# A two-layer retention and RWKV-7 backbone on one core: the values' products of each scan half step issued behind the products of the half step in front, in one PSUM bank for a pair of heads

## The chip, the cores and the metric

The kernel runs on one core of a Trainium2 chip. The metric is the device time of one execution in microseconds (us). The kernel before took 2461.8 us, the median of 3 runs (2458.17 to 2465.19).

## The reference

Two layers work on 1024 latent tokens and 256 context tokens of width 1024. Each layer normalizes, projects once to 4224 columns, runs two groups of heads, and sends both through one output projection. The group that matters here is the delta rule scan, 8 heads of 64 channels, in two directions, context first and then latents:

```python
def rwkv7_scan(r, w, k, v, kap, a, s0, reverse):
    def step(s, inp):
        r_t, w_t, k_t, v_t, kap_t, a_t = inp
        s_kap = jnp.einsum('bhvk,bhk->bhv', s, kap_t)
        s = (s * w_t[:, :, None, :]
             - s_kap[..., None] * (kap_t * a_t)[:, :, None, :]
             + v_t[..., None] * k_t[:, :, None, :])
        return s, jnp.einsum('bhvk,bhk->bhv', s, r_t)
    s_fin, y = lax.scan(step, s0, xs, reverse=reverse)
```

Around it, per layer:

```python
pl = hl @ w_in[layer]                       # and pc = hc @ w_in[layer] for the context
ret_l, ret_c = retention_branch(...)        # 8 retention heads, chunks of 128
rwo_l, rwo_c = rwkv_branch(...)             # the scan above, readout norm, bonus
mix_l = jnp.concatenate([ret_l * silu(gr_l), rwo_l * silu(gw_l)], axis=-1) @ w_out[layer]
xl = xl + g_l[:, None] * mix_l
```

## The kernel before

The scan is done in chunks. The 1280 tokens are 10 tiles of 128, the 8 heads are 4 pairs, so a layer has 40 steps (pair p, step s), and a step has two half steps of 64 tokens (i = 0 and 1). Both heads of a pair (h) and both directions (d) go through a half step together.

`prep` and `prep2` (called by `ahead`, up to three steps ahead of the scan) make what a half step needs without the state: `own` and `bk` (decayed keys and queries), `gq` (masked products of them), `bt` (transposed keys), `z2` (the inverse of the chunk's triangle, by six levels of small f16 products in the PSUM tile `pinv`), and `uv`. `uv` holds the values of a chunk, loaded by DMA, in partitions 64 to 127, and has two buffers.

`seq` (L1046) runs the scan. A half step takes a PSUM bank `pseq`, of which there is one (`sq=1`), seen as four regions k = 0 to 3, and in the text below each of its six groups of four f32 products (two heads, two directions) is called a set:

- v, the values' part: `gq` times `uv` into region 0 (L1053)
- s, the state's part: `own` times the state `st` into region 0, which ACT copies to `w` (L1068)
- w: `z2` times `w` into region 1; ACT and DVE copy it to `uv`, partitions 0 to 63 (L1080, L1081)
- a second s set, `own` times `st` for the outputs, into region 3
- b: `bt` times `uv` into region 2, from which DVE makes the next state `st` (L1093, two instructions)
- y: `gq` times `uv` into region 3, which ACT or DVE adds to the outputs `ym` (L1102, L1098)

All but v go through the helper `more` and carry its line, L1061. The first product of a set v clears the bank's written bits, and `behind` keeps the others of the bank after it in PE's order. Since the bank is taken anew for each half step, set v waits until the reads of the half step in front (L1093, L1098, L1102) are over.

The v and the y and b products take 128 rows by 64 columns of the array (64 columns per head, tile shape 128*64 in the rows), the s and w products 64*64, and nearly everything else 128*128 or 64*128.

Everything else is filler between the half steps: projections (`pproj`, L493 to L495, three f16 products for each f32 one), the retention heads (`pss`, `pkt`), the output projection (`pout`, L821 to L823). The program is scheduled by the tile framework, which plays it through with its own estimates and gives each engine a fixed order; `seq` and `prep2` are given a lead of 1000 places (`tc.high_priority(offset=1000)`), and `deal` hands out filler so that it ends at given steps. Each engine then works through its order.

Between the layers `out_last` adds the last output blocks for the tile groups [0,1], [4,5,6,7], [3,8] and [2,9], turns the residual (`pxo`, L890), and `norm_chunk` spreads the norm factors (`prsb`, L345) and writes `h_hi` and `h_lo`, on which layer 1's first projections work.

```python
with tc.high_priority(offset=1000):
    st = seq(sp, stages.pop(g), stages.get(g + 1) if s + 1 < NT else None, st, ys)
ahead(g + LOOK + 1)
```

Of the kernel before, what the change touches and what calls it, by code (L numbers as in the profile page):

```python
# [125 lines left out]
def hybrid_kernel(ctx: ExitStack, tc: tile.TileContext, a: dict, out: bass.AP, dbg: dict | None = None):  # L126
    nc = tc.nc
# [11 lines left out]
    def bank(tag, name):  # L139
        return ps.tile([128, 512], F32, tag=tag, name=name, bufs=BANKS[tag])  # L140
# [6 lines left out]
    def behind(ins, first):  # L147
        tc.add_manual_dep(ins.ins, first.ins.name, mybir.DependencyInfo(mybir.DependencyClass.NoSync, mybir.DependencyReason.DATA),
                          reason="the first product of a bank clears its written bits")
# [15 lines left out]
    def x_tile(tb):  # L165
        t = ln_pool.tile([128, D], F32, tag="xt", name="xt", bufs=XTB)
        load(t, a["ctx"][0, 128 * tb:128 * tb + 128, :] if tb < 2 else a["x"][0, 128 * (tb - 2):128 * (tb - 2) + 128, :])
        return t
# [39 lines left out]
    at = {}  # L208
# [162 lines left out]
    h = None  # L371
    rss, xres = {}, {}

    for l in range(DEPTH):
# [53 lines left out]
        h = (hp.tile([128, 8, TOK], F16, name="h_hi"), hp.tile([128, 8, TOK], F16, name="h_lo"))  # L428
        h_hi, h_lo = h
        if l == 0:  # L430
            lp = ln_pool
            stage = [lp.tile([128, 8, 128 * len(tiles)], F32, name=f"xs{ci}") for ci, tiles in enumerate(LN_TILES)]
            for ci, tiles in enumerate(LN_TILES):
# [5 lines left out]
                for i, tb in enumerate(tiles):  # L439
                    t = x_tiles[tb] if tb < XTB else x_tile(tb)  # L440
# [7 lines left out]
                for k in range(8):  # L448
                    p = bank(("inv", "m")[k % 2], "pxt")
# [457 lines left out]
        HR = [slice(0, 64), slice(64, 128)]  # L907
# [42 lines left out]
        def prep2(sp, c):  # L950
# [89 lines left out]
            nc.scalar.copy(z2, q)  # L1040
            c.update(gq=gq, bt=bt, z2=z2)

        def seq(sp, cur, nxt, st, ys):
            s, uv, gq, bt, z2, own = cur["s"], cur["uv"], cur["gq"], cur["bt"], cur["z2"], cur["own"]
            if s == 0:
                st = sp.tile([128, 2, 64], F32, tag="st", name="st", bufs=3)  # L1046
                nc.gpsimd.memset(st, 0.0)
            for i in range(2):
                pq = bank("sq", "pseq").rearrange("p (k d t) -> p k d t", k=4, d=2)
                first = []  # L1050
                for d in range(2):
                    for h in range(2):
                        wm = nc.tensor.matmul(pq[HR[h], 0, d, :], gq[:, h, i, d, 0:64], uv[:, i, d, 64 * h:64 * h + 64],  # L1053
                                              start=(d == 0), stop=False, skip_group_check=True)
                        if d == 0:
                            first.append(wm)
                        else:
                            behind(wm, first[h])

                def more(k, h, d, lhs, rhs, stop=False):  # L1060
                    rm = nc.tensor.matmul(pq[HR[h], k, d, :], lhs, rhs, start=False, stop=stop, skip_group_check=True)  # L1061
                    behind(rm, first[h])

                for d in range(2):
                    for h in range(2):
                        more(0, h, d, own[HR[h], i, d, 0:64], st[HR[h], d, :], True)
                w = sp.tile([128, 2, 64], F32, tag="w", name="w", bufs=2)
                nc.scalar.copy(w, pq[:, 0])  # L1068
                for d in range(2):
                    for h in range(2):  # L1070
                        more(1, h, d, z2[HR[h], i, d, :], w[HR[h], d, :], True)
                nf = cur["f"][:, 1, :] if i == 0 else (nxt["f"][:, 0, :] if nxt is not None else None)
                if nf is not None:
                    sf = sp.tile([128, 2, 64], F32, tag="sf", name="sf", bufs=1)
                    nc.gpsimd.tensor_tensor(sf, st, nf.unsqueeze(2).to_broadcast([128, 2, 64]), ALU.mult)
                for d in range(2):
                    for h in range(2):
                        if not cur["skip_y"]:
                            more(3, h, d, own[HR[h], i, d, 64:128], st[HR[h], d, :])
                nc.scalar.copy(uv[0:64, i, :, 0:64], pq[0:64, 1])  # L1080
                nc.vector.tensor_copy(uv[0:64, i, :, 64:128], pq[64:128, 1])  # L1081
                for d in range(2):
                    for h in range(2):
                        if nf is not None:
                            more(2, h, d, bt[:, i, d, 64 * h:64 * h + 64], uv[:, i, d, 64 * h:64 * h + 64], True)
                for d in range(2):
                    for h in range(2):
                        if not cur["skip_y"]:
                            more(3, h, d, gq[:, h, i, d, 64:128], uv[:, i, d, 64 * h:64 * h + 64], True)
                if nf is not None:  # L1090
                    st = sp.tile([128, 2, 64], F32, tag="st", name="st", bufs=3)
                    for d in range(2):
                        nc.vector.scalar_tensor_tensor(st[:, d, :], pq[:, 2, d, :], nf[:, d:d + 1], sf[:, d, :], ALU.mult, ALU.add)  # L1093
                if not cur["skip_y"]:
                    for d in range(2):
                        m, c = orders[d][s], (i if d == 0 else 1 - i)
                        if (m, c) in ys:
                            nc.vector.tensor_tensor(ys[m][:, c, :], pq[:, 3, d, :], ys[m][:, c, :], ALU.add)  # L1098
                        else:
                            if m not in ys:  # L1100
                                ys[m] = sp.tile([128, 2, 64], F32, tag="ym", name="ym", bufs=10)
                            nc.scalar.copy(ys[m][:, c, :], pq[:, 3, d, :])  # L1102
                        ys[(m, c)] = True
            return st
# [152 lines left out]
        for p in range(NP):  # L1257
            st, ys = None, {}
            for s in range(NT):
                g = p * NT + s  # L1260
# [3 lines that stand above are left out]
                if s == 1 and not last:  # L1264
                    need(p, gated)
                    readout(sp, p, s, 0, 1, ys)
                if s >= 6:
                    need(p, gated)
                    readout(sp, p, s, 11 - s, s, ys)
                deal(g)  # L1270
                while p == NP - 1 and not fills and todo and max(todo[0]) <= max(s, 1 if s < 7 else 7):
                    out_last(todo.pop(0))
# [43 lines left out]
```

## Time and profile before

| what | value |
|---|---|
| median of 3 runs | 2461.8 us (2458.17 to 2465.19) |
| the profiled execution | 2462.74 us |
| its span, first to last instruction | 2460.7 us |
| mean granted TensorE clock | 0.964 |
| busy: PE, DVE, ACT, POOL | 2299.2, 1735.6, 1414.8, 1319.7 us |
| products of the scan's sets in the trace (two records for each f32 product) | 1280 v, 2432 s, 1280 w, 1216 b, 1152 y |

The times of runs and of the profiled execution are of the whole device execution; the span leaves out 2.0 us around it. PE is TensorE, busy 93% of the span, and a busy PE may be one at half clock. The rows are times on one execution.

### The profile page before, as it was taken

How to read it: one execution, taken by the hardware profiler on the slowest of the kernel's cores; microseconds unless marked ns; L12 is line 12 of the kernel's file. 1: busy time of each engine (PE TensorE's matmuls, PEld its weight loads, DVE VectorE, ACT ScalarE, POOL GpSimd, SP SyncE). 2: the span in 40 equal slices, each digit the busy share in tenths (PEclk: the TensorE clock that was granted, in tenths of full speed). 3: DMA queues.
4: the chain of work that ended last, by engine and by line, in shares of the span. 5: the costliest groups of instructions: out<-in, count | busy, mean ns of one | idle time of the engine just before them, and what ended most of it. 6: DMA issues, size and time to landing. Idle time of an engine off the chain costs nothing.

```text
span 2460.7 us, 69593 instructions
## 1 busy us (share of the span) xinstructions
PE 2299.2 (93%) x25463; PEld 1739.9 (71%) x25463; DVE 1735.6 (71%) x4784; ACT 1414.8 (57%) x4261; POOL 1319.7 (54%) x2032
## 2 busy tenths in 40 slices
PE   5779999999999999999997899999999999998997
PEld 2357776877788777778655687778768877776855
DVE  2646686787678867777648677767867886669756
ACT  3455664565566655456546666646655665456663
POOL 1455564465556654456536556545654665456662
PEclk7888999999999999999998899999999999999998
DMA  8754443334334423335533543434433443334544
GB/s 313 270 187 110 117 118 87 113 108 124 78 89 139 126 70 92 75 100 154 176 108 123 152 130 112 108 94 119 128 87 100 124 124 80 79 88 120 143 130 128
DMA packets 539606, 302.77 MB, mean 123 GB/s; under 512 B 238995, under 2 KB 526465, under 8 KB 537217
## 3 DMA queue, kind: packets, MB, share of 16 engines
q1 hardware_dynamic: 539264, 298.33, 42.1%
q8 instruction: 201, 3.29, 0.6%
q14 instruction: 141, 1.15, 0.2%
HBM read 212.21 MB, written 85.98 MB: 121 GB/s over the span
## 4 chain that ended last, share of the span: by engine, by line
PE 58%; DVE 13%; DMA 6%; ACT 4%; issue 3%; POOL 2%; SPq 2%; DVEq 0%; POOLq 0%; ACTq 0%
PE pproj L493 8%; PE pproj L495 8%; PE pproj L494 8%; PE pseq L1061 8%; PE pm L962 5%; DMA ft<-feat 2%; PE pseq L1053 2%; PE pinv L1001 2%; PE pinv L1017 2%; PE pout L821 1%; PE pout L823 1%; PE pss L638 1%; PE pout L822 1%; PE pss L648 1%; PE pyt L1127 1%
## 5 line engine op out<-in xcount | busy, mean ns | idle before, releaser
L493 PE MATMUL pproj<-h_hi,whi 128*128 128x256 f16 (+2 forms) x2128 | 631.3, 298 | 9.1 <-ACT craw L505 5.1
L494 PE MATMUL pproj<-h_lo,whi 128*128 128x256 f16 (+2 forms) x2128 | 629.1, 297 | 7.6 <-DVE h_lo L365 7.1
L495 PE MATMUL pproj<-h_hi,wlo 128*128 128x256 f16 (+2 forms) x2128 | 627.2, 297 | 0.7 <-POOL wlo L320 0.7
L320 POOL TENSOR_TENSOR wlo<-wraw,whi 128x256 f16<-128x256 f32 x360 | 250.5, 707 | 208.7 <-ACT wraw L319 181.0
L495 PEld LDWEIGHTS <-wlo 128*128 128x128 f16 x2128 | 213.5, 100 | 76.5 <-issue 12.1
L494 PEld LDWEIGHTS <-whi 128*128 128x128 f16 x2128 | 212.6, 100 | 77.6 <-issue 18.6
L493 PEld LDWEIGHTS <-whi 128*128 128x128 f16 x2128 | 213.1, 100 | 75.3 <-issue 10.4
L986 POOL COPY ttb<-tt 64x256 f16<-64x256 f16 x320 | 139.1, 436 | 205.2 <-DVE tt L1021 160.5
L1015 DVE TENSOR_TENSOR xx<-pinv,lvm 128x256 f16<-128x256 f32 x400 | 164.3, 416 | 90.6 <-PE pinv L1001 87.4
L318 ACT ACTIVATE whi<-wraw 128x256 f16<-128x256 f32 x360 | 139.2, 412 | 132.9 <-PE pproj L494 61.1
L1018 ACT CAST tz<-pinv 128x256 f16<-128x256 f32 x400 | 146.1, 370 | 119.9 <-PE pinv L1017 107.7
L962 PE MATMUL pm<-own,bk 64*128 64x128 f32 (+1 forms) x1280 | 201.6, 294 | 8.3 <-DVE bk L942 4.0
L1021 DVE STREAM_TRANSPOSE tt<-tz 128x256 f16<-128x256 f16 x320 | 139.4, 437 | 97.0 <-ACT tz L1018 94.3
L976 POOL TENSOR_TENSOR il<-gq,c_id 64x256 f32<-64x256 f32 x160 | 120.1, 751 | 133.1 <-DVE gq L965 119.3
L986 ACT COPY ttb<-tt 64x256 f16<-64x256 f16 x320 | 128.6, 402 | 106.5 <-DVE tt L1021 102.1
L962 PEld LDWEIGHTS pm<-own,bk 64*128 64x128 f32 x1280 | 163.2, 193 | 33.1 <-issue 8.6
L965 DVE TENSOR_TENSOR gq<-pm,c_m 128x256 f32<-128x256 f32 (+1 forms) x320 | 115.7, 402 | 50.6 <-PE pm L962 49.8
L1061 PE MATMUL pseq<-st,own 64*64 64x64 f32 x2432 | 149.4, 228 | 0.0
L319 ACT ACTIVATE wraw<-wraw 128x256 f32<-128x256 f32 x376 | 146.3, 410 | 3.9
L1001 PEld LDWEIGHTS <-hi 128*128 128x128 f16 x1920 | 104.6, 99 | 41.6 <-issue 9.7
L1012 POOL TENSOR_TENSOR lo<-il,hi 64x256 f16<-64x256 f32 x160 | 113.5, 710 | 36.8 <-ACT hi L977 28.0
L1008 POOL TENSOR_TENSOR ttb<-hi,lvm 128x256 f16<-128x256 f16 x160 | 113.6, 729 | 19.0 <-ACT hi L977 18.2
(255 smaller groups left out, 5906.7 us busy)
## 6 DMA issues: line engine op xcount, KB each, us to landing
ft<-feat SPq DMA_DIRECT2D x320, 160.0 KB
wraw<-in_w_in_dram SPq DMA_DIRECT2D x264, 128.0 KB
feat<-zth SPq DMA_DIRECT2D x80, 256.0 KB
wm<-in_w_mod_dram SPq DMA_DIRECT2D x16, 1024.0 KB
wraw<-in_w_out_dram SPq DMA_DIRECT2D x112, 128.0 KB
lap<-la SPq DMA_DIRECT2D x40, 256.0 KB
uv<-vt SPq DMA_DIRECT2D x320, 32.0 KB
wm<-in_w_mod_dram SPq DMA_DIRECT2D x16, 512.0 KB
```

The source lines that it names most:

```text
L319: nc.scalar.activation(raw, raw, AF.Copy, scale=WS)
L320: nc.gpsimd.tensor_tensor(lo, raw, hi, ALU.subtract)
L493: nc.tensor.matmul(p[:, 0:n], hi[:, k, :], h_hi[:, kk, m0:m1], start=first, stop=False)
L494: nc.tensor.matmul(p[:, 0:n], hi[:, k, :], h_lo[:, kk, m0:m1], start=False, stop=False)
L495: nc.tensor.matmul(p[:, 0:n], lo[:, k, :], h_hi[:, kk, m0:m1], start=False, stop=stop)
L962: nc.tensor.matmul(pm[h][:, i, d, 0:q1], bk[HR[h], i, d, :], own[HR[h], i, d, 0:q1], start=True, stop=True)
L986: eng(idr(dst[HR[h], :, :, 64 * h:64 * h + 64]), idr(src[HR[h]]))
L1001: nc.tensor.matmul(q[:, i, d, :], hi[:, i, d, :], id16 if n == 0 else tz[:, i, d, :], start=True, stop=True)
L1015: nc.vector.tensor_tensor(xx, q, mk, ALU.mult)
L1018: nc.scalar.copy(tzn, tp)
L1021: nc.vector.transpose(idr(tt), idr(tzn))
L1061: rm = nc.tensor.matmul(pq[HR[h], k, d, :], lhs, rhs, start=False, stop=stop, skip_group_check=True)
```

## The change

A function `v_part` issues set v. Where the half step has a successor in the same pair of heads, it issues the successor's set v right behind its own set y, with the successor's `gq` and `uv` (of the next step where i is 1). The successor then uses the same `pseq` tile: the bank is taken once for a pair of heads, in its first half step, and set v there stands where it stood. The order on PE is held by `behind`: set v comes after all other products of the half step whose bank it clears. Region 0, into which v writes, was last read by the copy to `w`.

```diff
+        def v_part(pq, c, i, done):
+            first = []
+            for d in range(2):
+                for h in range(2):
+                    wm = nc.tensor.matmul(pq[HR[h], 0, d, :], c["gq"][:, h, i, d, 0:64], c["uv"][:, i, d, 64 * h:64 * h + 64],
+                                          start=(d == 0), stop=False, skip_group_check=True)
+                    if d == 0:
+                        first.append(wm)
+                        for rm in done[h]:
+                            behind(wm, rm)
+                    else:
+                        behind(wm, first[h])
+            return first
...
             for i in range(2):
-                pq = bank("sq", "pseq").rearrange("p (k d t) -> p k d t", k=4, d=2)
-                first = []
-                for d in range(2):
-                    for h in range(2):
-                        wm = nc.tensor.matmul(pq[HR[h], 0, d, :], gq[:, h, i, d, 0:64], uv[:, i, d, 64 * h:64 * h + 64],
-                                              start=(d == 0), stop=False, skip_group_check=True)
-                        if d == 0:
-                            first.append(wm)
-                        else:
-                            behind(wm, first[h])
+                if s == 0 and i == 0:
+                    at["pq"] = bank("sq", "pseq").rearrange("p (k d t) -> p k d t", k=4, d=2)
+                    at["first"] = v_part(at["pq"], cur, 0, ((), ()))
+                pq, first, done = at["pq"], at["first"], ([], [])
...
                     rm = nc.tensor.matmul(pq[HR[h], k, d, :], lhs, rhs, start=False, stop=stop, skip_group_check=True)
                     behind(rm, first[h])
+                    done[h].append(rm)
...
                             more(3, h, d, gq[:, h, i, d, 64:128], uv[:, i, d, 64 * h:64 * h + 64], True)
+                if nf is not None:
+                    at["first"] = v_part(pq, *((cur, 1) if i == 0 else (nxt, 0)), done)
                 if nf is not None:
                     st = sp.tile([128, 2, 64], F32, tag="st", name="st", bufs=3)
```

In the changed kernel set v has line L1048 and `more` has L1070. The number of instructions that do work is the same on every engine; the built order is not, since the framework schedules the whole program anew.

The first place is PE's order in the second half step of layer 0's first step, with the sets b and y and what follows them. Before:

```order
L993 MATMUL pinv<-z_2315,eb_1780 128x64
L1061 MATMUL pseq<-uv,bt 64x64 x4
L1061 MATMUL pseq<-uv,gq 64x64 x4
L962 MATMUL pm_3347<-own,bk 128x128 x4
L725 LDWEIGHTS wz
```

and 27 rows later the next half step's sets v and s:

```order
L1001 LDWEIGHTS hi_1773
L1001 MATMUL pinv<-id_96,hi_1773 128x64
L1053 MATMUL pseq<-uv,gq 64x64 x4
L1061 MATMUL pseq<-st,own 64x64 x4
L962 MATMUL pm_3354<-own,bk 128x128 x4
```

The same place in the changed kernel:

```order
L993 MATMUL pinv<-z_2315,eb_1780 128x64
L1070 MATMUL pseq<-uv,bt 64x64 x4
L1070 MATMUL pseq<-uv,gq 64x64 x4
L1048 MATMUL pseq<-uv,gq 64x64 x4
L962 MATMUL pm_3348<-own,bk 128x128 x4
```

and 26 rows later set s alone:

```order
L1001 LDWEIGHTS hi_1773
L1001 MATMUL pinv<-id_96,hi_1773 128x64
L1070 MATMUL pseq<-st,own 64x64 x4
L1001 LDWEIGHTS hi_1772
L1001 MATMUL pinv<-tz,hi_1772 128x64
```

Set v has moved from in front of s to behind y; s stands as far behind b as it did.

The second place is PE's order of the changed kernel some 460 rows on, two steps later, where f16 products (`pinv`) are put between the sets:

```order
L1070 MATMUL pseq<-uv,bt 64x64 x4
L1070 MATMUL pseq<-uv,gq 64x64 x3
L1001 LDWEIGHTS hi_1773
L1001 MATMUL pinv<-tz,hi_1773 128x64
...
L1070 MATMUL pseq<-uv,gq 64x64
L1017 LDWEIGHTS ttb_1786
L1017 MATMUL pinv<-xx,ttb_1786 128x64
...
L1048 MATMUL pseq<-uv,gq 64x64 x4
L495 LDWEIGHTS wlo
```

Here v follows y only after another group of f16 products.

The third place is PE's order between the layers, from the norm factors of the tile group [4,5,6,7] (`prsb`, four products) to those of [2,9]. Before, the four stand 6 `pout` products in front of layer 1's first `pproj`, and the two of [2,9] in front of the first `pproj` of the second piece of tokens (128x258):

```order
L345 MATMUL prsb<-c_id,rs 128x128 x4
L821 LDWEIGHTS wlh
...
L890 MATMUL pxo<-c_id,x_20197 128x128 x6
L493 LDWEIGHTS whi
L493 MATMUL pproj<-h_hi,whi 128x256
...
L890 MATMUL pxo<-c_id,x_20197 128x128 x4
L345 MATMUL prsb<-c_id,rs 128x128 x2
L493 LDWEIGHTS whi
L493 MATMUL pproj<-h_hi,whi 128x258
```

In the changed kernel three of the four stand 30 `pout` products in front of the first `pproj`, the factors of [3,8] 12 `pout` in front of it, and those of [2,9] behind 48 `pproj` of the second piece:

```order
L345 MATMUL prsb<-c_id,rs 128x128 x3
L821 LDWEIGHTS wlh
...
L345 MATMUL prsb<-c_id,rs 128x128
L890 MATMUL pxo<-c_id,x_20131 128x128 x2
...
L890 MATMUL pxo<-c_id,x_20131 128x128
L345 MATMUL prsb<-c_id,rs 128x128 x2
L890 MATMUL pxo<-c_id,x_20131 128x128 x4
...
L890 MATMUL pxo<-c_id,x_20131 128x128 x2
L493 LDWEIGHTS whi
L493 MATMUL pproj<-h_hi,whi 128x256
```

More output products stand behind the factors of the middle tiles, and the last tile pair's factors are out of the way of the projections.

## Rows read from the trace of the kernel before

**Rows 1.** The page's busy times, and PE with its clock in 40 slices.

```profile
PE 2299.2 (93%) x25463; PEld 1739.9 (71%) x25463; DVE 1735.6 (71%) x4784; ACT 1414.8 (57%) x4261; POOL 1319.7 (54%) x2032
...
PEclk7888999999999999999998899999999999999998
```

**Rows 2.** Windows by stage: stretch, length, busy of each engine, clock, DMA.

```profile
369.00:1180.00 811.00, 797.54 (x9332) 622.19 (x9331) 609.06 (x1766) 470.88 (x1446) 446.94 (x698) 0.99 0.38 105
1180.00:1440.00 260.00, 224.91 (x2121) 166.22 (x2120) 163.35 (x408) 150.63 (x438) 133.36 (x200) 0.93 0.45 134
1440.00:2214.00 774.00, 755.59 (x8700) 581.76 (x8698) 570.14 (x1611) 458.43 (x1398) 435.86 (x674) 0.99 0.39 106
```

**Rows 3.** PE's groups by line: busy, mean ns, idle before.

```profile
L1053 PE MATMUL pseq<-uv,gq 128*64 128x64 f32 x1280 | 80.1, 237 | 4.3 <-PE pinv L1017 0.9 <-PE pout L823 0.8 <-ACT ym L1102 0.7
L1061 PE MATMUL pseq<-uv,bt 128*64 128x64 f32 x1216 | 78.2, 237 | 7.0 <-DVE uv L1081 7.0
```

**Rows 4.** Timeline of PE at four places: start, us, what.

```profile
702.44 0.27 PE L495 MATMUL pproj<-h_hi,wlo 128*128 128x256 f16 x1
702.55 0.27 PE L493 MATMUL pproj<-h_hi,whi 128*128 128x256 f16 x1
702.75 0.45 PE L1053 MATMUL pseq<-uv,gq 128*64 128x64 f32 x8
703.13 0.45 PE L1061 MATMUL pseq<-st,own 64*64 64x64 f32 x8
703.51 0.28 PE L494 MATMUL pproj<-h_lo,whi 128*128 128x256 f16 x1
...
934.93 0.45 PE L1061 MATMUL pseq<-st,own 64*64 64x64 f32 x8
935.31 0.28 PE L495 MATMUL pproj<-h_hi,wlo 128*128 128x256 f16 x1
...
2419.99 0.45 PE L1061 MATMUL pseq<-uv,bt 128*64 128x64 f32 x8
2420.27 0.40 PE L1061 MATMUL pseq<-uv,gq 128*64 128x64 f32 x8
2420.61 0.33 PE L890 MATMUL pxo<-c_id,x 128*128 128x128 f32 x1
```

**Rows 5.** Timeline behind that last place: DVE's state update, then sets v and s.

```profile
2421.06 0.47 DVE L1093 SCALAR_TENSOR_TENSOR st<-pseq,f,sf 128x64 f32<-128x64 f32 x2
...
2421.90 0.45 PE L1053 MATMUL pseq<-uv,gq 128*64 128x64 f32 x8
2422.28 0.45 PE L1061 MATMUL pseq<-st,own 64*64 64x64 f32 x8
```

**Rows 6.** Timeline, the last step's loads of values, and set y of the step before.

```profile
2392.68 2.37 SPq L920 DMA_DIRECT2D uv<-vt  x4
...
2414.18 0.40 PE L1061 MATMUL pseq<-uv,gq 128*64 128x64 f32 x8
```

**Rows 7.** Timeline of PE between the layers.

```profile
1321.87 0.66 PE L890 MATMUL pxo<-c_id,x 128*128 128x128 f32 x4 [3.29 <-ACT osq L892]
1328.18 1.23 PE L345 MATMUL prsb<-c_id,rs 128*128 128x128 f32 x4 [5.65 <-POOL rs L250]
1330.45 0.67 PE L493 MATMUL pproj<-h_hi,whi 128*128 128x258 f16 x2 [1.04 <-ACT h_hi L364]
1332.32 0.38 PE L494 MATMUL pproj<-h_lo,whi 128*128 128x258 f16 x1 [1.20 <-DVE h_lo L365]
```

**Rows 8.** Windows of 8 to 16 us in the dense part, then between the layers.

```profile
1032.00:1040.00 8.00, 6.34 (x93) 5.03 (x94) 7.60 (x27) 4.71 (x16) 3.57 (x6) 0.80 0.45 104
1040.00:1056.00 16.00, 16.00 (x129) 12.99 (x126) 8.63 (x23) 6.36 (x23) 5.89 (x10) 0.50 0.20 59
...
1320.00:1330.00 10.00, 1.88 (x8) 1.38 (x9) 9.97 (x15) 6.16 (x15) 6.53 (x7) 0.68 0.11 35
1330.00:1340.00 10.00, 8.31 (x48) 5.83 (x48) 10.00 (x25) 7.99 (x29) 6.82 (x11) 0.64 0.20 52
```

## The prediction

> **What bounds the kernel now.** I read the page's busy times first, then windows by stage, then what PE waits for, and last the timeline around the scan's sets. PE is busy 93% of the span and DVE 71% [rows 1]. In the two long stretches where the scan and the filler run together PE is busy 797.5 of 811 us and 755.6 of 774 us, at a granted clock of 0.99 [rows 2]. So the scan's chain of products and copies does not bound these stretches: its sets are taken out of a full queue of filler, and when they come earlier, filler comes later. What a change can win there is work of PE itself, or part of the 13.5 and 18.4 us that are idle. Between the layers it is otherwise: of 260 us PE is busy 224.9, at clock 0.93 [rows 2], and the idle time stands in a few places where PE waits for the norm.
>
> The wait that the change removes is small. In front of the v products PE was idle 4.3 us in all, and of this 0.7 us were put down to a `ym` copy [rows 3]. The framework had already put v so late in PE's order that the bank was free.
>
> **Part 1: shapes of the array, the main term.** Sets v, b and y have tile shape 128*64, sets s and w 64*64, the filler mostly 128*128. The timeline prices a change of shape [rows 4]. One set alone between f16 products takes 935.31 - 934.93 = 0.38 us from its start to the next start. Two sets of one shape, b and y, take 2420.61 - 2419.99 = 0.62 us, so the second costs 0.24. Two sets of two shapes, v and s, take 703.51 - 702.75 = 0.76 us: the change between them costs 0.14 more. A set alone thus pays about 0.14 for leaving its shape. For entering it there is 702.75 - 702.55 = 0.20 us from the last `pproj` to the set, against 0.11 between two `pproj`: 0.09.
>
> Before, a half step in whole sets is v s | w s | b y, with one change of shape inside a group. After, it is s | w s | b y v, with none: 0.62 + 0.24 for b y v and 0.38 for s, 1.24 us, against 0.76 + 0.62 = 1.38 us. That is 0.14 us for each of the 152 half steps that have a successor in their pair (19 of 20 in each of 8 pairs), 21.3 us if every group stood whole. It doesn't: over the whole order of the changed kernel only 108 of 160 sets v stand whole behind a product of y or b, while of the old ones 134 of 160 stood whole in front of s. In the second place shown, v is on its own and pays entry and exit. Going through both orders and counting neighbours of different tile shape gives 2246 changes before and 2174 after, 72 fewer. An entry at 0.09 and an exit at 0.14 make 0.12 each on the mean, so 72 x 0.12 = 8.6 us less on PE. The bounds: 72 x 0.09 = 6.5 us, and 72 x 0.14 = 10.1 us. As PE is the full engine, this shows in the span nearly whole.
>
> The Trainium skill, TensorEngine Tiling (Array Packing), Key Properties, says that changing the tiling mode drains TensorE and that another tile of the same mode doesn't. It has no price for it, and it speaks against this change wherever the scheduler leaves v alone: a set cut off from its group pays the drain twice. By the rule only the count of changes matters, and that count fell; by the rows the fall is worth what the sum above says.
>
> **Part 2: waits that go and come.** The wait for `ym` and the other readers goes: a gain from 0 to the 4.3 us of [rows 3]. I take 0, since other work was ready in most of these places in another order. Set s now waits for DVE's state update by itself, where the wait used to stand at v. In the place of [rows 5] set b started at 2419.99 [rows 4], the update ended at 2421.53, and s came at 2422.28, 0.75 us later; in both orders shown s stands some 30 rows behind b, so it is no nearer to the update than it was. I take 0; the upper bound is the nearest wait of this chain that does cost, b waiting for the copy to `uv`, 7.0 us in all [rows 3]. Queued behind a waiting s would be all filler of PE, and with it every copy of ACT and DVE that empties a bank.
>
> Set v at the end of a step now needs the next step's `uv` earlier, by the way from y to v (1.6 us from [rows 4] to [rows 5]). The last step's loads were all issued by 2395.05, and set y behind which v now goes started at 2414.18 [rows 6]: 19 us to spare. No cost. SP issues the same loads, held by the same release of `uv` (two buffers, last read by set y). Set v also writes into the bank while DVE and ACT may still read regions 2 and 3; set y did so before while DVE read region 2. In the order v waits only for the loads, so I take no cost.
>
> **Part 3: between the layers.** The framework scheduled everything anew, and one place looks better. Before, PE stops at the norm of the last tiles: 3.29 us for ACT, 5.65 us for the factors of [2,9] on POOL, then 1.04 and 1.20 us for `h_hi` and `h_lo`, 11.2 us in all [rows 7], with DVE full (9.97 of 10 us) and the clock at 0.68 and 0.64 in the 20 us from 1320 [rows 8]. The clock that is missing there, (1 - 0.68) x 10 + (1 - 0.64) x 10 = 6.8 us at full speed, costs PE up to that much more. In the new order the factors of [4,5,6,7] come 24 `pout` products earlier against the first `pproj` (30 in front of it, not 6), and those of [2,9] stand behind 48 more `pproj`, so they no longer stop work that could run. At 0.11 us a product, 24 `pout` and the transposes among them are some 3.5 us of PE work that now lies over DVE's norm. But DVE has five more residual adds in that stretch, and the norm itself, not PE, is the bound. I take 5 us of the 11.2 + 6.8 us: the 3.5 us of cover and a share of the clock. The bounds are 0 and 11 us.
>
> **Part 4: the end and the rest.** Less chain in the last half steps is worth little, since `pout` products fill PE there; I take 0.
>
> **Sum.** 2462.7 (the profiled execution) - 8.6 - 5 = 2449.1 us. The median of the runs, 2461.8, is 0.9 us below the profiled execution, which is inside their spread. I forecast 2449 us, 0.5% faster. Differences below 0.3%, 7.4 us, are about what a measurement of this kernel can't tell from no change (its runs spread over 7.0 us).
>
> **Rival A: no change that can be measured, 2458 us.** The shapes save 8.6 us of PE work, but PE meets as many new waits as it loses work, in a new order made from estimates and not from the chip, and the place between the layers stays as it was, since DVE's norm is full there either way. For it: DVE at 9.97 of 10 us [rows 8], and the 13.5 and 18.4 us of idle time that the old order left [rows 2], which a new one may double as well as halve. Half of part 1 remains: 2462.7 - 4.3 = 2458. That the bank is still guarded as a whole, so that v waits for `ym` as before, would give the same; the order speaks against it, v standing next to y. The Trainium skill, PSUM — Partial Sum Buffer, PSUM bank collisions raise a hardware error, asks for semaphores by bank and quadrant, and by it v would stand behind DVE's and ACT's reads; no row of the order shows such a wait, and I give it 0.03 of this rival's chance.
>
> **Rival B: slower, by set s waiting for the state.** If the chip's update comes later than the framework thought, PE stops at s in each half step. A mean stop of 0.2 us makes 152 x 0.2 = 30.4 us: 2449 + 30 = 2479 us. It decides against the change from 13.6 / 152 = 0.09 us, and makes it measurably slower from (13.6 + 7.4) / 152 = 0.14 us. Against it: 0.75 us to spare in a tight place at the end of the program [rows 5], and 30 rows of other work in the middle.
>
> **Rival C: the clock.** In the dense part, after 1.66 us of idle time within 8 us, the granted clock stood at 0.50 for 16 us with PE busy throughout [rows 8]: 8 us lost. A new order makes and unmakes such places. One more is 2449 + 8 = 2457, two more are 2465, one fewer is 2441.
>
> **How the numbers follow.** Forecast (2440 to 2454): 0.58. A: 0.22. C with one or two more drops: 0.10 (no measurable change). B or three drops: 0.10. Part of A's and C's chance lies just under the bound and part of the forecast's just over it. Faster 0.62, same 0.26, slower 0.12. The range goes down to 2462.7 - 10.1 - 11 - 4.3, about 2437, and one drop of the clock fewer, of which I take a part: 2434. Above it takes in A and most of C: 2465. The forecast's own range is 2440 to 2454.
>
> **What the changed profile would show.** Set v starts some 0.25 us behind y, and b, y and v take about 0.86 us from start to next start. PE's busy time falls by about 9 us. The idle time in front of v nearly goes, that in front of s stays below 3 us. The idle places at the norm factors between the layers add up to 6 us or less. I am wrong if PE waits for the state update at s in many half steps, if the wait at the norm is as long as before, or if the low clock takes up more of the dense stretches.

## The result and the profile after

The changed kernel takes 2491.2 us (median of 6 runs, 2485.25 to 2500.74), the kernel before beside it 2459.7 us: a ratio of 1.0128, 95% interval 1.0104 to 1.0151. It is 31.4 us slower. The profiled execution took 2500.74 us (span 2499.0 us, mean clock 0.952) and lies 9.6 us above its median.

The page's busy times and PE's clock in 40 slices, to be read beside [rows 1]:

```profile
PE 2319.7 (93%) x25463; PEld 1752.7 (70%) x25463; DVE 1720.6 (69%) x4784; ACT 1412.9 (57%) x4261; POOL 1318.5 (53%) x2032
...
PEclk7889999998999999999998899999999999988998
```

PE is busy 20.5 us longer with the same 25463 products, and slices with a clock below 0.9 stand where none stood, in layer 0's scan and near the end. Windows over the same steps of the scan as [rows 2]:

```profile
367.40:1191.60 824.20, 803.04 (x9298) 621.54 (x9296) 604.65 (x1765) 467.25 (x1445) 446.61 (x698) 0.98 0.38 103
1191.60:1459.40 267.80, 232.66 (x2164) 173.36 (x2162) 165.22 (x413) 152.22 (x439) 134.84 (x201) 0.92 0.45 133
1459.40:2237.60 778.20, 760.33 (x8722) 585.06 (x8721) 565.30 (x1614) 461.31 (x1408) 437.05 (x677) 0.98 0.38 105
```

The three stretches are 13.2, 7.8 and 4.2 us longer, and what follows the last of them to the end of the span is 14.7 us longer (2499.0 - 2237.6 against 2460.7 - 2214). The first of them and that end have 7.7 and 7.8 us more idle time; the other two have no more than before. PE's groups for the sets s, w, v and b (busy, mean ns, idle before them):

```profile
L1070 PE MATMUL pseq<-st,own 64*64 64x64 f32 x2432 | 148.8, 229 | 2.1 <-ACT ym L1114 1.2 <-DVE ym L1110 0.9
L1070 PE MATMUL pseq<-w,z 64*64 64x64 f32 x1280 | 83.5, 236 | 8.1 <-ACT w L1078 7.7
...
L1048 PE MATMUL pseq<-uv,gq 128*64 128x64 f32 x1280 | 83.1, 229 | 0.7 <-DMA uv<-vt 0.7
L1070 PE MATMUL pseq<-uv,bt 128*64 128x64 f32 x1216 | 76.9, 238 | 6.0 <-DVE uv L1091 5.8
```

Against [rows 3] the idle time in front of v has gone from 4.3 to 0.7 us and that in front of b from 7.0 to 6.0. The s sets wait 2.1 us, not for the state but for the copies to `ym`: three waits (1.18, 0.58 and 0.30 us), each in front of the first s set of a half step, which writes region 0, while the copies read region 3. The timeline of one half step, and DVE's state update behind it (start, us):

```profile
925.64 0.27 PE L494 MATMUL pproj<-h_lo,whi 128*128 128x256 f16 x1
925.84 0.45 PE L1070 MATMUL pseq<-uv,bt 128*64 128x64 f32 x8
926.12 0.40 PE L1070 MATMUL pseq<-uv,gq 128*64 128x64 f32 x8
926.36 0.40 PE L1048 MATMUL pseq<-uv,gq 128*64 128x64 f32 x8
926.69 0.28 PE L495 MATMUL pproj<-h_hi,wlo 128*128 128x256 f16 x1
...
926.81 0.47 DVE L1105 SCALAR_TENSOR_TENSOR st<-pseq,f,sf 128x64 f32<-128x64 f32 x2 [0.38 <-PE pseq L1048]
```

Set v starts 0.24 us behind y, and b, y and v take 926.69 - 925.84 = 0.85 us. The state update, which reads what b wrote, begins only when v is over, and so it does in all 152 half steps that have a successor; before, it waited for y or b. In both traces none of the 1072 reads of the bank by DVE and ACT overlaps a product into it: the program guards the bank as a whole and not by region.

Otherwise the sets do what was forecast. The time is lost elsewhere. For every kernel below the span is split into three parts: **idle** (span less PE's busy time on the page), **low clock** (half of PE's busy time in the stretches where the trace's clock records read 0.50, the lower of the two levels, 1.2 GHz) and **work** (the rest: PE's busy time, counted as at the full 2.4 GHz). Shape changes are counted in the trace between neighbouring products of PE.

| profiled execution | span | idle | low clock | work | shape changes |
|---|---|---|---|---|---|
| before | 2460.7 | 161.5 | 67.3 | 2231.9 | 2246 |
| changed | 2499.0 | 179.3 | 100.0 | 2219.6 | 2174 |
| difference | +38.3 | +17.8 | +32.7 | -12.2 | -72 |

Work fell, as forecast. Idle time and low clock rose by four times as much. (The split is of one execution each, and that of the changed kernel was the slowest of its six: by the medians the difference is 31.4 us, not 38.3.) From the first set of the scan to the last, without the stretch between the layers, there were 6 stretches at half clock before and there are 15 now; what they cost went from 25.9 to 51.6 us. One of the new ones, in the timeline (behind the bracket: idle time and what ended it) and in windows (length, PE busy, clock):

```profile
589.86 0.28 PE L1001 MATMUL pinv<-id,hi 128*128 128x64 f16 x4
592.59 0.69 PE L664 MATMUL pot<-c_id,ob 128*128 128x128 f32 x2 [2.45 <-DVE ob L661]
```

```profile
570.00:590.00 20.00, 19.42 (x249) 1.00 0.60 162
590.00:606.00 16.00, 13.55 (x82) 0.57 0.42 119
606.00:626.00 20.00, 20.00 (x219) 1.00 0.29 84
```

A retention head's transpose waits 2.45 us for DVE, and over the 16 us around and behind it the mean clock is 0.57. Neither instruction has to do with set v.

Between the layers PE stops in other places than in [rows 7] (timeline from 1331 to 1364 us, the rows that waited longer than 0.4 us):

```profile
1334.63 0.66 PE L890 MATMUL pxo<-c_id,x 128*128 128x128 f32 x4 [1.70 <-ACT osq L892]
1337.05 0.37 PE L821 MATMUL pout<-mh,wlh 128*128 128x256 f16 x1 [1.76 <-DVE x L824]
1342.98 0.48 PE L890 MATMUL pxo<-c_id,x 128*128 128x128 f32 x1 [2.79 <-DVE x L824]
1348.92 0.27 PE L494 MATMUL pproj<-h_lo,whi 128*128 128x258 f16 x1 [1.33 <-DVE h_lo L365]
1350.74 0.27 PE L494 MATMUL pproj<-h_lo,whi 128*128 128x258 f16 x1 [0.47 <-DVE h_lo L365]
1358.38 0.27 PE L493 MATMUL pproj<-h_hi,whi 128*128 128x258 f16 x1 [2.18 <-ACT h_hi L364]
1360.94 0.38 PE L494 MATMUL pproj<-h_lo,whi 128*128 128x258 f16 x1 [2.29 <-DVE h_lo L365]
```

The wait for the factors of [2,9] is gone, and 12.5 us of waits for residual adds and `h_hi`, `h_lo` stand in place of the 11.2. In the whole stretch between the layers PE is idle 35.1 us, as before.

Near the end stands the longest new stop of the scan's own chain, in front of set w:

```profile
2448.97 0.69 PE L1070 MATMUL pseq<-w,z 64*64 64x64 f32 x8 [4.15 <-ACT w L1078]
```

### The profile page after: what moved, and what is told of

The parts are those of the page before. It is cut to its first block, busy times and chain, and to the rows that moved or that the text cites. A ratio compares the mean times of both kernels' runs of the same rounds, so it can differ in the third digit from the quotient of the medians.

```text
span 2499.0 us, 69412 instructions
## 1 busy us (share of the span) xinstructions
PE 2319.7 (93%) x25463; PEld 1752.7 (70%) x25463; DVE 1720.6 (69%) x4784; ACT 1412.9 (57%) x4261; POOL 1318.5 (53%) x2032
## 5 line engine op out<-in xcount | busy, mean ns | idle before, releaser
L494 PE MATMUL pproj<-h_lo,whi 128*128 128x256 f16 (+2 forms) x2128 | 634.0, 300 | 10.5 <-DVE h_lo L365 10.2
L320 POOL TENSOR_TENSOR wlo<-wraw,whi 128x256 f16<-128x256 f32 x360 | 247.2, 697 | 236.4 <-ACT wraw L319 188.5
L494 PEld LDWEIGHTS <-whi 128*128 128x128 f16 x2128 | 214.9, 101 | 80.3 <-issue 20.8
L1070 PE MATMUL pseq<-st,own 64*64 64x64 f32 x2432 | 148.8, 229 | 2.1 <-ACT ym L1114 1.2
L1070 PEld LDWEIGHTS pseq<-st,own 64*64 64x64 f32 x2432 | 107.4, 137 | 28.6 <-issue 7.4
```

The costliest lines, as they stand in the source:

```text
L320: nc.gpsimd.tensor_tensor(lo, raw, hi, ALU.subtract)
L494: nc.tensor.matmul(p[:, 0:n], hi[:, k, :], h_lo[:, kk, m0:m1], start=False, stop=False)
```

## The experiments

### The order and the place of set v, apart

Theory 1: the new order of everything else makes the loss. Theory 2: the place of set v and the kept bank make it. Since the framework orders the whole program anew for any edit, both orders were written down and held, by an edge without a wait from each instruction to the next on its engine. With its own order held the kernel before is, row for row and wait for wait, the same program as built. Set v was then moved alone.

```diff
+def hold_order(nc, tc):
+    ...
+    for c in _COUNTS:               # PE, DVE, ACT, POOL, SP
+        q = ns[o:o + c]             # numbers of instructions in the order to be held
+        o += c
+        for a, b in zip(q, q[1:]):
+            tc.add_manual_dep(nc.find_inst_by_name(f"I-{b}"), f"I-{a}",
+                              mybir.DependencyInfo(mybir.DependencyClass.NoSync, mybir.DependencyReason.DATA),
+                              reason="held order")
...
         hybrid_kernel(tc, args, outs[0])
+        hold_order(nc, tc)
```

**Old order, set v behind y.** 

> The changed code (set v behind y, one bank for a pair of heads), but all five engines held to the order of the kernel before, in which only the sets v are taken out and put right behind the last product of b and y of the half step in front. Theory 1 (the loss of 31.4 us is made by the new order of everything else; set v behind y is a gain by itself): PE's work falls by at least the 12.2 us that the changed kernel's trace shows, no cluster of idle time or drop of the clock is new, so 2459.7 - 12 = about 2448 us, 2443 to 2454. Theory 2 (the loss is made by where set v stands and by the bank that is kept, so that reads and writes of one bank run into each other or the scan's chain stops the filler): about as slow as the changed kernel, 2491 us, 2480 to 2500, with PE idle in front of set s or v. If both have a part: in between.

Measured: 2433.4 us (2429.44 to 2438.59), ratio 0.9911 (0.9883 to 0.9939). The change is a gain of 22 us in the old order, the fastest kernel of this study. Theory 2 falls, and Theory 1's 2448 us was 15 us too high: it took the fall of work from the changed kernel, and in the old order, with every set v whole behind y, work falls by more. Its page, windows over the same steps, and groups:

```profile
PE 2272.5 (93%) x25463; PEld 1727.0 (71%) x25463; DVE 1732.0 (71%) x4784; ACT 1414.2 (58%) x4261; POOL 1322.0 (54%) x2032
...
PEclk7789999999999999999998899999999999998998
```

```profile
368.20:1164.00 795.80, 779.31 (x9328) 610.13 (x9327) 605.21 (x1765) 470.57 (x1445) 448.46 (x697) 1.00 0.39 107
1164.00:1419.00 255.00, 224.69 (x2136) 166.83 (x2134) 163.71 (x411) 150.25 (x438) 133.67 (x200) 0.93 0.46 136
1419.00:2184.80 765.80, 745.97 (x8691) 576.98 (x8691) 568.09 (x1609) 458.39 (x1398) 435.32 (x673) 0.99 0.39 107
```

```profile
L1070 PE MATMUL pseq<-st,own 64*64 64x64 f32 x2432 | 149.4, 228 | 2.6 <-DVE ym L1110 1.2 <-DVE st L1105 0.8 <-ACT ym L1114 0.5
...
L1048 PE MATMUL pseq<-uv,gq 128*64 128x64 f32 x1280 | 71.6, 227 | 0.2 <-issue 0.2
```

The dense stretches are 15.2 and 8.2 us shorter than in [rows 2], at clocks of 1.00 and 0.99. PE's busy time is 26.7 us below [rows 1], and 8.5 us of that show at set v itself (80.1 us in [rows 3]). The split is idle 161.8, low clock 71.1, work 2201.4, with 2053 shape changes: 193 changes and 30.4 us of work fewer, idle time as before. The later state update shows here too, with all else in the old order: from the end of b to the update it takes 0.81 us in the median, before 0.65. It costs little, since s starts 2.4 us behind the update in the median; 0.8 us of PE's idle time are put down to it.

**New order, set v in front of s.** 

> The code of the kernel before (set v in front of s, the bank taken for each half step), but all five engines held to the order of the changed kernel, in which only the sets v are taken out and put right in front of the first set s of their own half step. Theory 1: the order keeps its idle time and its drops of the clock, and PE gets the 12.2 us of work back: 2491 + 12 = about 2503 us, 2490 to 2515. Theory 2: the loss is gone with the place of set v, 2460 us, 2452 to 2470.

Measured: 2488.5 us (2486.62 to 2491.64), ratio 1.0138 (1.011 to 1.0165). Theory 2 falls: with v back in its place and the bank taken anew the kernel is as slow as the changed one. Theory 1's 2503 was too high by 14 us, and the time lies just below its range (by the ratio, on the 2459.7 us of the kernel before, it is 2494). Work rose to 2230.0 us as expected (2242 changes), but idle time (174.2) and low clock (85.5) of that execution were lower than the changed kernel's. The stop in front of w near the end is there as well, so it belongs to the order and not to set v:

```profile
2438.85 0.69 PE L1061 MATMUL pseq<-w,z 64*64 64x64 f32 x8 [3.80 <-ACT w L1068]
```

**New order, set v gathered.** 

> The changed kernel, held to its own order on all engines, except that each set v which its order had torn apart or put off stands whole right behind the last product of b and y of the half step in front (152 sets, 108 before). Theory 1: only PE's work falls, by some 0.16 us for each change of shape less (the first experiment: 30.4 us for 193 changes), about 60 changes or 10 us; the new order's idle time and low clock stay: about 2480 us, 2472 to 2492, far above the 2433 us of the old order with the same sets. Theory 2b (the torn sets v are what made the new order slow): 2455 us or less.

Measured: 2479.8 us, ratio 1.0079 (1.0049 to 1.0108), as Theory 1 had it. Work 2204.0 us at 2087 changes, idle 178.2, low clock 104.7 (the slowest of its four executions): the torn sets cost PE 15.6 us of work, and the order keeps its idle time and its low clock.

**The kept bank alone.** 

> One part of the change alone: one bank for a pair of heads, but set v issued where it was, in front of s, with all engines held to the order of the kernel before. Theory 1: the kept bank costs nothing and gains nothing beyond the idle time in front of v, 4.3 us at most: 2450 to 2462 us. Theory 2 (the kept bank makes part of the loss, by reads and writes of one bank at one time): 2470 us or more.

```diff
                 if s == 0 and i == 0:
                     at["pq"] = bank("sq", "pseq").rearrange("p (k d t) -> p k d t", k=4, d=2)
-                    at["first"] = v_part(at["pq"], cur, 0, ((), ()))
+                    at["done"] = ((), ())
+                at["first"] = v_part(at["pq"], cur, i, at["done"])
                 pq, first, done = at["pq"], at["first"], ([], [])
+                at["done"] = done
...
-                if nf is not None:
-                    at["first"] = v_part(pq, *((cur, 1) if i == 0 else (nxt, 0)), done)
```

Measured: 2452.6 us (2447.81 to 2463.57), ratio 0.9974 (0.9953 to 0.9996). The kept bank costs nothing, and may be 1 to 12 us of the gain of the first experiment. Since this kernel has set v where it was and the old order held, it shows as well that holding an order costs nothing. Its idle time was 147.1 us, 14.4 below that of the kernel before in the same order: idle time of a single execution is no finer than that.

### Other orders of the same work

One number of the plan was changed, in the kernel before and in the changed one. The work stays the same, the order does not. A line by line comparison of PE's 50,926 rows in the traces (products and weight loads, without line and buffer numbers) against the kernel's own plan as it was has 20,300 to 38,000 lines that differ, counted on both sides, for the kernel before and 5,300 to 37,800 for the changed one, and 41,000 between these two.

```diff
-RAMP = 5.0
+RAMP = 5.5                                    # or 6.5
-DENSE = ((447.0, 113.0), (403.0, 88.0))
+DENSE = ((450.0, 113.0), (406.0, 88.0))       # or 444.0 and 400.0
-                with tc.high_priority(offset=1000):
+                with tc.high_priority(offset=900):     # or 1100, for seq and prep2
```

RAMP 5.5, before: 

> The kernel before with one number of its plan of filler changed by a tenth (RAMP 5.0 to 5.5), which gives another order of the same work (about as many rows of PE stand elsewhere as in the changed kernel) with set v where it was. Theory 1, in which any new order of this program costs PE idle time and clock: slower than 2459.7 us by 10 to 40 us. Theory 2: the same time within 8 us.

RAMP 5.5, changed: 

> The changed kernel with RAMP 5.5 for 5.0: another order with set v behind y, to be set beside the kernel before with the same edit (2485.5). Theory 1: some 12 us below its partner, give or take the spread of orders of 15 us: 2455 to 2490. Theory 2: above its partner by as much as the change cost, 31 us: about 2515.

DENSE up, before: 

> The kernel before with the planned cost of the filler of the scan set 3 us higher in either layer (447 to 450, 403 to 406 us), which gives another order of the same work from layer 0's scan on, about half as many rows of PE elsewhere as in the changed kernel, with set v where it was. Theory 1: slower than 2459.7 us by 5 to 30 us. Theory 2: the same time within 8 us.

DENSE up, changed: 

> The changed kernel with the planned cost of the filler 3 us higher in either layer: another order with set v behind y, to be set beside the kernel before with the same edit (2473.6). Theory 1: some 12 us below its partner, give or take 15 us: 2447 to 2480. Theory 2: about 31 us above it, 2505.

Lead 900, before: 

> The kernel before with the lead of seq and prep2 at 900 places in place of 1000: the same work in another order, set v where it was. Theory 1 (the order before is a good one of many, and any other one costs idle time and clock): 2465 to 2490 us. Theory 2 (the order doesn't matter by itself): within 8 us of 2456.

Lead 900, changed: 

> The changed kernel with the lead of seq and prep2 at 900 places in place of 1000: set v behind y, another order. Theory 1: the time is another draw from the same spread as those of the re-ordered kernels with v in the old place (2474 and 2486 so far), less some 12 us of PE work for the place of v: 2455 to 2490, and not systematically at 2491. Theory 2 (the place of v and the kept bank cost time in any order that the framework makes): 2485 to 2500.

Lead 1100, before: 

> The kernel before with the lead of seq and prep2 at 1100 places: another order, set v where it was. By either theory of the orders (below, its partner) 2456 to 2490 us.

Lead 1100, changed: 

> Partner of the kernel before with a lead of 1100 places, set v behind y. Theory 1a (how good an order comes out is chance; the four pairs so far, +31, +17, +15 and -12 us, are a draw): the differences of the new pairs scatter about -12 us (PE's work), -30 to +10. Theory 1b (with set v put behind y the framework makes looser orders as a rule, PE idle some 8 us more in the dense part in all four so far): the new pairs are +5 to +30 us like most before. This kernel's order is near that of the changed kernel (a seventh as many rows elsewhere as between the two kernels), so 2480 to 2495 us by both.

DENSE down, before: 

> The kernel before with the planned cost of the filler 3 us lower in either layer (444 and 400): another order, set v where it was. 2456 to 2490 us by either theory of the orders.

DENSE down, changed: 

> Partner of the kernel before with the planned cost 3 us lower, set v behind y. Theory 1a (chance): 30 us below to 10 us above its partner. Theory 1b (looser orders as a rule): 5 to 30 us above it, with PE idle some 8 us more in the dense part.

RAMP 6.5, before: 

> The kernel before with RAMP 6.5: another order, set v where it was. 2456 to 2490 us by either theory of the orders.

RAMP 6.5, changed: 

> Partner of the kernel before with RAMP 6.5, set v behind y. Theory 1a (chance): 30 us below to 10 us above its partner. Theory 1b (looser orders as a rule): 5 to 30 us above it, with PE idle some 8 us more in the dense part.

Measured, medians in us with the ratio to the kernel before, and the differences (v behind y less v in front of s) of the two profiled executions:

| plan | v in front of s | v behind y | ratio, difference | idle | low clock | work |
|---|---|---|---|---|---|---|
| as it was | 2459.7, 1 | 2491.2, 1.0128 | +1.28% | +17.8 | +32.7 | -12.2 |
| RAMP 5.5 | 2485.5, 1.0116 | 2502.7, 1.0157 | +0.41% | +8.9 | +25.4 | -7.9 |
| DENSE up | 2473.6, 1.0086 | 2488.2, 1.0112 | +0.26% | +10.0 | +15.2 | -13.7 |
| lead 900 | 2467.4, 1.0029 | 2455.9, 0.9985 | -0.44% | +15.3 | -0.7 | -25.5 |
| lead 1100 | 2472.0, 1.0064 | 2485.9, 1.0106 | +0.42% | +17.2 | +10.5 | -16.7 |
| DENSE down | 2459.9, 1.0003 | 2479.9, 1.0099 | +0.96% | +17.7 | +25.7 | -25.3 |
| RAMP 6.5 | 2475.4, 1.0064 | 2464.2, 1.0009 | -0.55% | +1.5 | +21.0 | -22.4 |
| mean | 1.0052 | 1.0085 | +0.33% | +12.6 | +18.5 | -17.7 |

With set v in its old place, seven orders of one program spread over 1.2%. The order before is the best of them together with DENSE down (1.0003), 0.52% better than their mean; whether it is so by choice or by luck is not on record. The changed kernel's order is 0.43% worse than the mean of its seven. So by the means, of the 1.28% some 0.33% belong to the change as the framework orders it, with the wide interval below, and 0.95% to these two orders.

The theories of the single runs: RAMP 5.5 and DENSE up, with v in its old place, refute that the order doesn't matter (1.0116 and 1.0086), and DENSE down refutes that any new order costs time. The changed kernels of RAMP 5.5 and DENSE up came out slower than Theory 1 had them (2502.7 and 2488.2 us against 2490 and 2480 at most) and short of Theory 2's 2515 and 2505; lead 900 lay where Theory 1 had it. Of the last pairs DENSE down and lead 1100 went as 1b had it, and RAMP 6.5 as 1a.

Chance or a rule? The seven differences have a mean of +0.33% with a 95% interval of 0.62 to either side. No loss as a rule is shown by that, but the gain of 12 us (-0.5%) that Theory 1a needed is outside. (Without the first pair, which raised the question, the mean is +0.18%, with 0.60 to either side.) Work fell in seven pairs of seven, idle time rose in seven and low clock in six: as a rule, the framework's orders with v behind y leave more idle time on PE (12.6 us on the mean, with 5.6 to either side). Its places in the changed kernel are spread over the program: the waits that grew most are those of `pinv` for a copy by DVE (L1004, 1.0 to 8.8 us), of set w for ACT's copy (0.9 to 7.7) and of `pproj` and `pout` for weights split by POOL (L320, 1.3 to 7.0). Why the framework's estimates lead there stays open.

### The price of a stop

Two kernels add waits to the first experiment's kernel, in the same order: a weight load of PE waits for an instruction of POOL that ends a little later.

```diff
+def stalls(nc, tc):
+    for x, z in _STALLS:            # a product of PE, an instruction of POOL
+        tc.add_manual_dep(nc.find_inst_by_name(f"I-{x}"), f"I-{z}",
+                          mybir.DependencyInfo(mybir.DependencyClass.Sync, mybir.DependencyReason.DATA),
+                          reason="stall")
```

**Ten long stops.** 

> The kernel of the first experiment (old order, set v behind y: 2433 us, its profiled execution 2436.1), with one wait more at ten places of the dense part, at least 100 us apart: a weight load of PE waits there for an instruction of POOL that in the first experiment's trace ended 1.9 to 2.1 us after the load's product began. Work and order stay the same; 20.2 us of stops in all. Theory 1, in its second half (a stop of some 2 us makes the granted clock fall to half behind it, and that costs more than the stop): 20 us and 1.7 to 5 us of clock for each place, 2433 + 20 + 10 x 3.4 = about 2487 us, 2470 to 2505, with some ten half-clock stretches more than in the first experiment. Rival: a stop costs its own length or less, since it takes the place of later waits: 2443 to 2455 us, with the clock as before.

Measured: 2473.5 us, ratio 1.0054 (1.0028 to 1.008), 40 us above the first experiment (35 by the ratios). In the trace the ten places take 20.8 us longer from the product in front to the next. One of them, in the timeline and in windows:

```profile
507.44 0.27 PE L495 MATMUL pproj<-h_hi,wlo 128*128 128x258 f16 x1
509.70 0.28 PE L493 MATMUL pproj<-h_hi,whi 128*128 128x258 f16 x1 [2.00 <-POOL wlo L320]
```

```profile
490.00:508.00 18.00, 17.71 (x212) 1.00 0.31 87
508.00:532.00 24.00, 22.30 (x160) 0.57 0.27 76
532.00:550.00 18.00, 18.00 (x219) 1.00 0.40 110
```

PE was busy all the while before it and behind it, and after this one stop of 2.00 us the clock stood at half for 20.5 us. Five of the ten places were followed by half clock, together 37.5 us with PE busy throughout, 18.7 us lost. 20.8 + 18.7 = 39.5 us is near the loss by the medians, but not the whole account: against the first experiment's profiled execution the split is +23.6 us of idle time, +7.7 of low clock and +1.7 of work, 33.0 in all, since half-clock stretches that stood elsewhere in that execution are missing in this one. The time is in the range of Theory 1 and the rival's 2443 to 2455 falls; five new stretches came, not ten, and 1.9 us of clock a place on the mean, not 3.4.

**Forty short stops.** 

> As the ten long stops, but with forty places at least 30 us apart, where PE waits for an instruction of POOL that ended 0.4 to 0.6 us after the product began: 17.9 us of stops in all, nearly the same sum as that of the ten long ones. Theory 1: spread so thinly they leave the clock alone, so that they cost 18 us or less: 2440 to 2455 us, and the ten long ones cost 20 us and more than these. Rival (only the sum of idle time counts): the same time as the ten long stops within 6 us.

Measured: 2451.9 us, ratio 0.9959 (0.9935 to 0.9983), 18.5 us above the first experiment (12 by the ratios). The places take 19.3 us longer, most of them like this:

```profile
531.49 0.27 PE L493 MATMUL pproj<-h_hi,whi 128*128 128x258 f16 x1
532.06 0.28 PE L494 MATMUL pproj<-h_lo,whi 128*128 128x258 f16 x1 [0.29 <-POOL ttb L986]
```

```profile
530.00:536.00 6.00, 5.71 (x72) 1.00 0.47 143
```

None of the forty was followed by half clock. The two kernels ran beside each other, and the ten long stops took 21.6 us more than the forty short ones with nearly the same sum: the rival, that only the sum counts, falls. Of the two profiled executions the one with long stops has 19.2 us more low clock.

## Why the prediction was wrong

**What bounds the kernel**: right for the two dense stretches, where PE is full. But what changed the time was not PE's work.

**Part 1 (shapes, -8.6 us)**: right, and a little too small. Work fell by 12.2 us for 72 changes of shape, and by 30.4 us for 193 in the old order, 0.16 to 0.17 us a change; a straight line through the work and the changes of all twenty profiled executions gives 0.15 (95% interval 0.13 to 0.17) with a scatter of 3 us, so 0.12 was low. The mean over an entry at 0.09 and an exit at 0.14 left out part of what a change costs. The Trainium skill, TensorEngine Tiling (Array Packing), Key Properties, says that a change of mode drains TensorE; these runs agree.

**Part 2 (waits, 0)**: right for v, s and b. The idle time in front of v fell by 3.6 us, s waited 2.1 us and b 6.0; only w, with 7.7 us on ACT's copy, waits longer, and with v back in its place in the new order it does too (7.0). One reason of this part was wrong: "set y did so before while DVE read region 2". No product into the bank overlapped a read of it, before or after; the bank is guarded as a whole, which rival A named and set aside, and the price is that the state update now stands behind v, and s, not v, behind the copies to `ym`. **Rival B** is refuted all the same: no order here shows more than 0.9 us of idle time put down to the state update in front of s.

**Part 3 (between the layers, -5 us)**: wrong. The stop at the factors went as forecast, and 12.5 us of stops at the residual adds and the norm came for 11.2. DVE's norm was the bound, as the argument said itself. It was a term taken from one place of a new order, where the rest of that order was counted as nothing.

**Part 4 (the end, 0)**: wrong. What follows the dense stretches is 14.7 us longer, with 7.8 us more idle time, and among its stops is one of 4.15 us in front of a set w. The new order makes this stop with v in its old place as well (3.80 us).

**The step that failed** is the sum's silence on the order: "The framework scheduled everything anew, and one place looks better." The sum has a term for that one place and puts the rest of the order at nothing. **Rival C** named one half of the mechanism, the clock, with a price of 8 us for a drop that PE's work follows, and gave "one or two more drops" 0.10 and "three drops" part of another 0.10. There were nine more while the scan ran, most of them shorter (25.7 us of low clock), with 17.8 us more idle time in the whole span, the half that rival A had as "as many new waits as it loses work". That new order is what made the kernel slow: held to the old one, it gains 22 us; held to the new one with v put back, the kernel before is as slow.

**What the changed profile would show**: v's 0.25 us, the 0.86 us and the idle time in front of v and s came. PE's busy time did not fall by 9 us, the stops at the norm stayed above 6 us, and the last named sign of being wrong came: "the low clock takes up more of the dense stretches".

## What to carry to other kernels

Where a framework orders the whole program, an edit is two changes: its own, and a new order of everything. Cost the second by a spread (here seven orders of one program lie within 1.2%, and a kernel whose order is among the best of them loses 0.5% on the mean by a new one), and measure the first with the order held. Then keep the order, as the kernel of the first experiment does, 0.9% faster than the one before. When PE is full, count its stops by size: here ten of some 2 us cost nearly as much again in clock, and nearly the same sum in pieces of about half a microsecond cost no more than itself.

## What the runs showed of the hardware

A single stop of PE of 1.8 to 2.1 us was followed by half clock in five places of ten; in one of these the clock stayed there for 20.5 us with PE busy throughout. Forty stops of up to 0.64 us, 30 us apart, never were. A change of the array's tile shape costs 0.15 us of PE's time over the twenty profiled executions (0.13 to 0.17), and 0.16 to 0.18 by pairs of them (30.4 us for 193, 12.2 for 72, 27.9 for 159). The mean granted clock of one program is not fixed: in 14 executions of the kernel before it went from 0.959 to 0.972, with 2467.8 us at the one and 2444.5 us at the other.
